# Differential scores: a second product over all 128 rows with zeros beside the keys' low parts, and a distance table loaded for each head

## The chip, the cores and the metric

The kernel runs on one core of a Trainium2 chip. The metric is the device time of one execution in microseconds (us): lower is better. Engines are named as the profile names them: PE (TensorE products), PEld (TensorE loads of the stationary operand, which lie beside PE), DVE (VectorE), ACT (ScalarE), POOL (GpSimd), SP (SyncE, which here only issues transfers; SPq is its queue).

## The reference, cut to what matters

A first block (adaptive norm, SSD and gated delta scans) is followed by a second block of two layers. Each layer projects 512 tokens of width 2048, runs a gated convolution, a differential attention and an attention to 256 memory tokens, and projects back. The change sits in the differential attention, six heads with two components of 64 features each:

```python
def diff_attention(q, k, v, lam, slopes):
    scale = DIFF_HALF_DIM ** -0.5
    ...
    def block(args):            # 128 queries
        qi, i = args
        qpos = (i * Q_BLOCK + jnp.arange(Q_BLOCK)).astype(jnp.float32)
        bias = -slopes[:, None, None] * jnp.abs(qpos[:, None] - key_pos[None, :])
        sc = jnp.einsum('bhcqd,bhckd->bhcqk', qi, kt).astype(jnp.float32) * scale + bias[None, :, None]
        p = jax.nn.softmax(sc, axis=-1).astype(vt.dtype)
        o = jnp.einsum('bhcqk,bhkd->bhcqd', p, vt)
        return o[:, :, 0] - lam.astype(o.dtype) * o[:, :, 1]
```

## The kernel before, in words

Products are made in the one-pass format float32r with operands split in two: a high part and a low part that holds what the high one leaves out. A projection takes three products for each tile: high by high, low by high, high by low. Weights come in pieces of 512 KB (128x1024) or 384 KB (128x768) through SP into `wr` (three buffers, `wpiece`); ACT makes the high part `wh` and DVE the low part `wl` (two buffers each); SP issues the next load when the `wl` of three pieces earlier is done. The order on each engine is fixed when the program is built.

In block 2 a layer (`layer`) runs two groups of three heads. For a group, `qk_group` projects the queries and then the keys of three heads token-major (`tm`), norms them, turns them feature-major (`qkT`) and stacks them for the scores: tile `q0` or `q1` (component c) holds the component's 64 query features' high parts in its own 64 rows (0 to 63 for c = 0, 64 to 127 for c = 1) and the low parts in the other 64; `k0` or `k1` holds the keys' high parts twice. One tile `kl` holds the low parts of both components' keys, each in its own rows. `v_group` makes the values.

`diff_head` then takes four chunks of 128 queries (qc). For a chunk and a component it issues two products into one PSUM tile `sc`: one over all 128 rows ([q high; q low] with [k high; k high]) and one over the component's 64 rows (q high with k low):

```python
nc.tensor.matmul(sc, lhsT=q[c][:, qs], rhs=k[c], start=True, stop=False)
nc.tensor.matmul(sc, lhsT=q[c][cs, qs], rhs=k[2][cs, :], start=False, stop=True)
```

So a chunk has a block of four score products on PE, and there are 2 layers x 6 heads x 4 chunks = 48 blocks. DVE adds the distance bias and takes the maximum (`p<-sc,bias`, with `mx`), ACT takes the exponentials, DVE combines the two components (`p<-p,c`). PE transposes the result (`pT`), ACT copies it out (`pTe`) and PE multiplies it with the values (`pv`); these steps are emitted one and two chunks later (`defer`), and in each chunk half a feature tile of other work (24 products `fm`, lines 176 to 178) is put between (`fill`). PSUM has four tiles for these (`g`) and four for projections (`mm`).

The bias of a head is a 128x896 tile with one buffer: POOL multiplies a resident table of distances (`dist`, loaded once from the constants `cst`) with the head's slope. Its buffer comes free when DVE has read the last chunk of the head before.

`mem_attention` reuses the tiles `k0`, `k1`, `q0`, `q1` for the memory's keys and values (`mk`, `mv`) and the tile `qktm` for its own queries.

Of the kernel before, what the change touches and what calls it, by code (L numbers as in the profile page):

```python
# [19 lines left out]
P = 128  # L20
# [5 lines left out]
# how far ahead of their place in the program the weights of each part are loaded and split  # L26
AHEAD = {"ada": 200, "mem": 300, "A": 300, "z": 300, "S": 300, "C": 150, "o1": 300, "tm": 300, "fm": 300, "o2": 300}
# half tiles of z projected at each place of block 1 where other work has waits to fill
ZFILL = {"keys": 2, "keys end": 2, "head": 1, "group": 2, "pair": (2, 2, 2, 4)}
# half tiles of the feature-major projection at each place of a layer's attention  # L30
FFILL = {"q": 2, "k": 2, "queries": 1, "mem q": 2, "mem queries": 1}
# adaLN steps before the constants, the memory's projections and the latent stream's loads come in
# [36 lines left out]
def lay_out(inp):  # L69
    """Orders the inputs for the chip: reshapes, transposes, concatenations and copies only."""  # L70
# [50 lines left out]
class K:  # L121
    def __init__(self, tc, I, out):
        self.tc, self.nc, self.I, self.out = tc, tc.nc, I, out
        # queues of the stores and of the loads of what was stored
        self.st, self.ld = tc.nc.scalar, tc.nc.sync
        self.queue = []
        self.part = "A"

    # ---------------------------------------------------------------- helpers
# [3 lines left out]
    def defer(self, *steps):  # L133
        """Emits the next step of each piece deferred so far, and takes the steps of a new one: what a step
        needs has time to come while other work is emitted in between."""
        self.advance()
        self.queue.append(list(steps))
# [29 lines left out]
    def proj_fm(self, outs, src, m=P, halves=(0, 1)):  # L167
        """ps[m, tok] = sum_k W[k, m] x[k, tok] for each (ps, x hi, x lo); src [2, P, 8*m]."""
# [11 lines left out]
    def proj_tm(self, pss, src, g, xh, xl):  # L180
        """pss[t][tok, g] = sum_k x[k, tok] W[k, g]; src [8, P, 2*g]."""
# [29 lines left out]
    def rsqrt_small(self, out, src, scale, n):  # L211
        """out = (src*scale + eps)^-0.5 on a small tile: a guess from the bits, a Newton and a Halley step."""
# [8 lines left out]
        # Newton's step leaves kappa times its value, so that Halley's needs no factor  # L221
# [12 lines left out]
    # ---------------------------------------------------------------- setup  # L234
    def first(self, out, src):
        """Load ahead of everything else."""
        with self.tc.high_priority(4000):
            self.nc.sync.dma_start(out=out, in_=src)
# [16 lines left out]
    def constants(self):  # L255
        """Constants and parameters of block 1, the lambda of the differential attention."""
# [19 lines left out]
        # halved convolution taps and bias (silu(x) = (tanh(x/2) + 1) * x/2)  # L276
# [18 lines left out]
    def rstd_cols(self, sq, n, width, out):  # L295
        """out[P, n/128] = (sum over partitions of sq / width + eps)^-0.5, tokens on partitions; sq may be parts of a sum."""
# [9 lines left out]
    def rstd_bcast(self, sq, n, width, out, cols=None):  # L306
        """out[P, n] = (sum over partitions of sq / width + eps)^-0.5, the same in every partition."""
        self.rstd_rows(self.rstd_diag(sq, n, width, self.tmp("rdiag")[:, :n], cols), out)

    def rstd_diag(self, sq, n, width, dg, cols=None):  # L310
        """rstd_cols in diagonal matrices."""
# [14 lines left out]
    # ---------------------------------------------------------------- adaLN  # L326
# [19 lines left out]
    def ada_chunk(self, cch):  # L346
        """Columns cch*1024 .. of the modulation of both streams, as per-partition columns (in steps)."""
        nc = self.nc
        pss = [self.psum("ch", "ada") for _ in range(2)]
        for k in range(KT):  # L350
            # one piece in four goes in whole, as float32: TensorE has the time, the split engines have not
# [29 lines left out]
    def gate_acc(self, i):  # L381
        """Partial sums over the features of quarter i of the latent stream's gate, c @ w_ada[:, 4096:]."""
# [12 lines left out]
    def gate_end(self, i, acc):  # L395
        """Columns of quarter i of the gate, times the post norm's gain."""
# [8 lines left out]
    # ---------------------------------------------------------------- memory keys and values  # L405
    def mem_prep(self):
        """hi and lo parts of the memory tokens and the columns of their norm, in steps."""
# [20 lines left out]
    def mem_proj(self, l, i, name):  # L428
        """Token-major product of the memory with block i of layer l's weights, whose rows take the norm's gain."""
# [22 lines left out]
    def mem_k(self, l):  # L452
        """Keys of the memory for layer l, feature-major, to DRAM, in steps."""
        nc = self.nc
        mkd = self.mkd[l] = self.dr.tile([P, 4, 256], F32, name=f"mkd{l}")
        # rms over the head in token-major form, then feature-major
# [24 lines left out]
    def mem_v(self, l):  # L481
        """Values of the memory for layer l, token-major, to DRAM, in steps."""
# [11 lines left out]
    # ---------------------------------------------------------------- modulated input of block 1  # L494
    def load_x(self):
        """Both streams and the sums of their squares, in steps."""
# [12 lines left out]
    def modulation(self):  # L509
        """The modulated inputs of both streams, in steps."""  # L510
# [23 lines left out]
    def modulate(self, half):  # L534
# [6 lines left out]
        if half == 0:  # L541
            # the context's tiles come first, so that theirs are the first places to be taken again
# [18 lines left out]
    def _affine(self, x, k, s):  # L561
        """x * (1 + scale) * gain + shift of feature tile k of stream s, in place."""
        self.nc.vector.tensor_scalar(out=x, in0=x, scalar1=self.am[:, k, s:s + 1], scalar2=self.mod[:, k, s:s + 1], op0=MUL, op1=ADD)

    # ---------------------------------------------------------------- block 1
    def targets(self, phs, name):
        """PSUM tiles of one projection for the given phases."""
        return [(self.psum("mm", name)[:, :ph.tok], ph.uh, ph.ul) for ph in phs]

    def small_proj(self, outs):  # L570
        """The 64 narrow outputs: rows 0-63 take W hi x hi + W hi x lo, rows 64-127 W lo x hi."""
# [17 lines left out]
    def tables(self, ph, ps):  # L589
        """Decay tables of one phase, token-major [P, column, chunk], and their rows."""  # L590
# [20 lines left out]
        # log1p(t) = 2 atanh(s), s = t / (2 + t)  # L611
# [42 lines left out]
        # dt * decay to the chunk's end (SSD columns)  # L654
# [1080 lines left out]
```

## Time and profile before

| | us |
|---|---|
| median of 3 runs | 3385.19 |
| lowest and highest run | 3374.1 and 3385.48 |
| span of the profiled execution, first to last instruction | 3380.9 |
| median of the runs less that span | 4.3 |

The profiled execution's own time is not listed apart from its span; the runs that are shown lie between 6.8 us below and 4.6 us above it. The page of the profile gives each engine's busy time in the span, and queries of the trace give single instructions with their start, their length and what they waited for. On PE the recorded lengths overlap, since products are pipelined: the time that one costs is the distance from its start to the next start.

### The profile page before, as it was taken

Reading aid. Unit: us, or ns where it says so; the run is one execution under the profiler, and the core shown is the slowest. Engines: PE = TensorE matmul, PEld = TensorE weight load, DVE = VectorE, ACT = ScalarE, POOL = GpSimd, SP = SyncE. Lnnn points to the kernel's source line nnn. Section 1 sums busy time; section 2 is a strip of 40 time slices with the busy share of each in tenths; the row PEclk is TensorE's granted clock in tenths of the full one; section 3 lists DMA queues with packets and bytes.
Section 4 is the critical chain, followed back from the end, with each engine's and each line's share of the span. In section 5 each row is a group of like instructions: output and inputs, shape, how many; then the busy total and the mean of one; then the engine's idle time right before and its main releaser. Section 6 shows DMA issues by size and latency. Waiting matters only on the chain.

```text
span 3380.9 us, 43409 instructions
## 1 busy us (share of the span) xinstructions
PE 3231.7 (96%) x16218; PEld 2665.5 (79%) x16218; DVE 1971.8 (58%) x3709; ACT 1228.0 (36%) x2371; POOL 481.8 (14%) x492
## 2 busy tenths in 40 slices
PE   7979989999999999997999999999999999999999
PEld 4637877787887887776888978888899798788887
DVE  7788887768667667666544464444344635544522
ACT  5644433334333333223333343323233434333311
POOL 1021220303424324012100010000110101000000
PEclk8989999999999999998999999999999999999999
DMA  8842342322322232754322322223433133122343
GB/s 313 283 172 86 130 134 84 107 99 89 106 77 70 79 103 76 251 186 143 103 79 74 115 73 88 76 93 131 146 109 108 57 101 110 63 88 81 107 149 106
DMA packets 169459, 392.57 MB, mean 116 GB/s; under 512 B 42784, under 2 KB 45344, under 8 KB 169248
## 3 DMA queue, kind: packets, MB, share of 16 engines
q1 hardware_dynamic: 140976, 341.02, 30.8%
q10 hardware_dynamic: 24432, 42.48, 3.3%
q0 software_dynamic: 3840, 6.29, 0.8%
q8 instruction: 128, 2.10, 0.3%
q14 instruction: 83, 0.68, 0.1%
HBM read 340.96 MB, written 42.47 MB: 113 GB/s over the span
## 4 chain that ended last, share of the span: by engine, by line
PE 52%; DVE 1%; issue 0%; ACT 0%; DVEq 0%; ACTq 0%
PE fm L178 7%; PE fm L176 7%; PE fm L177 7%; PE tm L192 4%; PE tm L191 4%; PE tm L190 4%; PE o L178 3%; PE o L177 3%; PE o L176 3%; PE pv L1490 2%; PE sc L1508 1%; PE sc L1507 1%; PE pT L209 1%; PE msc L1575 0%; PE qkT L1454 0%; PE oT L209 0%
## 5 line engine op out<-in xcount | busy, mean ns | idle before, releaser
L154 ACT CAST wh<-wr 128x1024 fp32r<-128x1024 f32 (+1 forms) x448 | 449.5, 1004 | 1328.5 <-PE fm L177 374.3
L155 DVE TENSOR_TENSOR wl<-wr,wh 128x1024 fp32r<-128x1024 f32 (+1 forms) x448 | 556.2, 1242 | 567.2 <-ACT wh L154 561.7
L176 PE MATMUL fm<-xh,wh 128*128 128x512 f32 x1088 | 431.5, 397 | 1.2 <-ACT qktm L1433 1.2
L178 PE MATMUL fm<-xh,wl 128*128 128x512 f32 x1088 | 426.1, 392 | 0.0
L177 PE MATMUL fm<-xl,wh 128*128 128x512 f32 x1088 | 425.1, 391 | 0.0
L192 PE MATMUL tm<-wh,xl 128*128 128x384 f32 (+1 forms) x896 | 308.3, 347 | 10.9 <-DVE xl L1409 10.7
L190 PE MATMUL tm<-wh,xh 128*128 128x384 f32 (+1 forms) x896 | 309.8, 346 | 3.9 <-ACT xh L1408 3.9
L191 PE MATMUL tm<-wl,xh 128*128 128x384 f32 (+1 forms) x896 | 308.6, 345 | 0.0
L176 PE MATMUL o<-yh,wh 128*128 128x512 f32 x768 | 299.7, 391 | 3.3 <-ACT yh L154 2.0
L178 PE MATMUL o<-yh,wl 128*128 128x512 f32 x768 | 299.8, 391 | 3.0 <-DVE wl L155 3.0
L177 PE MATMUL o<-yl,wh 128*128 128x512 f32 x768 | 299.6, 390 | 0.9 <-DVE yl L155 0.9
L178 PEld LDWEIGHTS fm<-xh,wl 128*128 128x128 f32 x1088 | 204.4, 188 | 42.9
L176 PEld LDWEIGHTS fm<-xh,wh 128*128 128x128 f32 x1088 | 204.6, 188 | 42.1 <-ACT qktm L1433 2.0
L177 PEld LDWEIGHTS fm<-xl,wh 128*128 128x128 f32 x1088 | 204.7, 188 | 39.8
L713 DVE SCALAR_TENSOR_TENSOR cacc<-cx,hcw,cacc 128x496 f32<-128x496 f32 (+2 forms) x248 | 165.4, 678 | 70.4 <-ACT cacc L706 67.2
L192 PEld LDWEIGHTS tm<-wh,xl 128*128 128x128 f32 x896 | 168.9, 189 | 20.5 <-DVE xl L1409 15.4
L190 PEld LDWEIGHTS tm<-wh,xh 128*128 128x128 f32 x896 | 169.7, 189 | 10.7 <-ACT xh L1408 5.5
L191 PEld LDWEIGHTS tm<-wl,xh 128*128 128x128 f32 x896 | 169.7, 189 | 4.8
L178 PEld LDWEIGHTS o<-yh,wl 128*128 128x128 f32 x768 | 144.2, 188 | 35.1 <-DVE wl L155 5.5
L176 PEld LDWEIGHTS o<-yh,wh 128*128 128x128 f32 x768 | 144.1, 188 | 34.7 <-ACT yh L154 3.4
L177 PEld LDWEIGHTS o<-yl,wh 128*128 128x128 f32 x768 | 144.2, 188 | 32.5 <-DVE yl L155 2.8
L176 PE MATMUL qkv<-uh,wh 128*128 128x512 f32 x384 | 154.8, 403 | 2.3 <-ACT wh L154 2.3
(523 smaller groups left out, 6229.7 us busy)
## 6 DMA issues: line engine op xcount, KB each, us to landing
wr<-w_fm SPq DMA_DIRECT2D x136, 512.0 KB
wr<-w_in SPq DMA_DIRECT2D x104, 512.0 KB
wr<-w_tm SPq DMA_DIRECT2D x96, 384.0 KB
ar<-w_ada SPq DMA_DIRECT2D x64, 512.0 KB
wr<-w_o SPq DMA_DIRECT2D x64, 512.0 KB
wr<-w_mkv SPq DMA_DIRECT2D x32, 512.0 KB
wr<-w_out SPq DMA_DIRECT2D x32, 512.0 KB
gw<-w_ada SPq DMA_DIRECT2D x64, 256.0 KB
```

The source lines that it names most:

```text
L154: nc.scalar.copy(hi, src)
L155: (eng or nc.vector).tensor_tensor(out=lo, in0=src, in1=hi.bitcast(F32), op=SUB)
L176: nc.tensor.matmul(ps, lhsT=hi[:, s], rhs=xh[kk], start=kk == 0, stop=False)
L177: nc.tensor.matmul(ps, lhsT=hi[:, s], rhs=xl[kk], start=False, stop=False)
L178: nc.tensor.matmul(ps, lhsT=lo[:, s], rhs=xh[kk], start=False, stop=kk == 15)
L190: nc.tensor.matmul(ps, lhsT=xh[kk][:, ts], rhs=hi[:, s], start=kk == 0, stop=False)
L191: nc.tensor.matmul(ps, lhsT=xh[kk][:, ts], rhs=lo[:, s], start=False, stop=False)
L192: nc.tensor.matmul(ps, lhsT=xl[kk][:, ts], rhs=hi[:, s], start=False, stop=kk == 15)
L209: self.nc.tensor.transpose(ps[:, m * P:(m + 1) * P], src[:, m * P:(m + 1) * P], self.C["ident"])
L713: nc.vector.scalar_tensor_tensor(out=av[:, :, o0:o1], in0=pv[:, :, o0 + d:o1 + d], scalar=w(k), in1=av[:, :, o0:o1], op0=MUL, op1=ADD)
L1490: self.nc.tensor.matmul(o[:, :P], lhsT=e[:, kc * P:(kc + 1) * P], rhs=v[kc][:, hs], start=kc == 0, stop=kc == n - 1)
L1507: nc.tensor.matmul(sc, lhsT=q[c][:, qs], rhs=k[c], start=True, stop=False)
```

## The change

The keys' low parts get a tile for each component (`kl0`, `kl1`, three buffers each), whose other 64 rows POOL sets to zero, and the second score product contracts all 128 rows: [q high; q low] with [k low; 0]. It takes the same stationary operand as the first. The resident table `dist` is gone; each head loads the distances into its own bias tile through SP (448 KB) and POOL multiplies them there in place. `qktm` shrinks to 384 columns, and the memory's queries move to the tiles `kl0` and `kl1`. The rest of the difference is comments.

```diff
@@ qk_group
-        tmt = self.wk.tile([P, 4, 512], F32, tag="qktm", name="qktm")[:, :, :384]
-        self.head_norm(pss, 6, 64, tmt)
+        tmt = self.wk.tile([P, 4, 384], F32, tag="qktm", name="qktm")
+        self.head_norm(pss, 6, 64, [tmt[:, t, :] for t in range(4)])
...
-            lo = self.wk.tile([P, 512], F32R, tag="t" if gain is None else "kl", name=f"{name}l")
+            if gain is None:
+                los = [self.wk.tile([P, 512], F32R, tag="t", name="ql")] * 2
+            else:
+                los = [self.wk.tile([P, 512], F32R, tag=f"kl{c}", name=f"kl{c}") for c in range(2)]
             for c in range(2):
-                r, o = slice(64 * c, 64 * c + 64), slice(64 - 64 * c, 128 - 64 * c)
+                r, o, lo = slice(64 * c, 64 * c + 64), slice(64 - 64 * c, 128 - 64 * c), los[c]
...
                     nc.gpsimd.dma_start(out=st[c][o], in_=st[c][r])
-            res.append((*st, lo))
+                    nc.gpsimd.memset(lo[o].bitcast(F32), 0.0)
+            res.append((st, los))
@@ diff_head
-        nc.gpsimd.tensor_scalar(out=bias, in0=self.dist, scalar1=-slope, scalar2=None, op0=MUL)
+        nm = len(NCONST) * P
+        nc.sync.dma_start(out=bias, in_=self.I["cst"][:, nm:nm + 896])
+        nc.gpsimd.tensor_scalar(out=bias, in0=bias, scalar1=-slope, scalar2=None, op0=MUL)
...
-                cs = slice(64 * c, 64 * c + 64)
                 sc = self.psum("g", "sc")
-                nc.tensor.matmul(sc, lhsT=q[c][:, qs], rhs=k[c], start=True, stop=False)
-                nc.tensor.matmul(sc, lhsT=q[c][cs, qs], rhs=k[2][cs, :], start=False, stop=True)
+                for i, kt in enumerate((k[0][c], k[1][c])):
+                    nc.tensor.matmul(sc, lhsT=q[0][c][:, qs], rhs=kt, start=i == 0, stop=i == 1)
@@ mem_attention
-        tma = self.wk.tile([P, 4, 512], F32, tag="qktm", name="mqtm")
-        tmt = [tma[:, t, :] for t in range(4)]
-        self.head_norm(pss, 4, P, tma)
+        tmt = [self.wk.tile([P, 512], F32, tag=f"kl{t % 2}", name="mqtm") for t in range(4)]
+        self.head_norm(pss, 4, P, tmt)
@@ block2
-            self.dist = cp.tile([P, 896], F32, name="dist")
-            self.nc.sync.dma_start(out=self.dist, in_=self.I["cst"][:, nm:nm + 896])
```

On PE no instruction changes its place; this is the difference at one chunk of the first layer's first head (`k_` tiles are the stacked keys of the two components, `kl` the low parts, `q_` the stacked queries, `vtm` the values):

```order
 L178 MATMUL fm<-xh,wl 128x512
-L1507 MATMUL sc<-k_14901,q_14516 128x512
-L1508 MATMUL sc<-kl,q_14516 128x512
-L1507 MATMUL sc<-k_14902,q_14517 128x512
-L1508 MATMUL sc<-kl,q_14517 128x512
-L1490 MATMUL pv<-vtm,pTe 128x128 x4
+L1514 MATMUL sc<-k_14899,q_14514 128x512
+L1514 MATMUL sc<-kl_14901,q_14514 128x512
+L1514 MATMUL sc<-k_14900,q_14515 128x512
+L1514 MATMUL sc<-kl_14902,q_14515 128x512
+L1495 MATMUL pv<-vtm,pTe 128x128 x4
 L209 MATMUL pT<-ident,p 128x128 x4
```

Four score products stand where four stood; only the tile of the low parts is another for each component.

On SP the loads of the table stand between loads of weights (`w_tm` and `w_fm` are pieces of the token-major and the feature-major projections); this is the difference over the first group of layer 0, from its beginning to the load for head 3:

```order
-L163 DMA wr<-w_fm 128x1024 x12
-L163 DMA wr<-w_tm 128x768 x8
+L163 DMA wr<-w_tm 128x768 x2
+L1503 DMA bias<-cst 128x896
+L163 DMA wr<-w_tm 128x768 x6
+L163 DMA wr<-w_fm 128x1024 x2
+L163 DMA wr<-w_tm 128x768 x8
+L163 DMA wr<-w_fm 128x1024 x8
+L1503 DMA bias<-cst 128x896
+L163 DMA wr<-w_fm 128x1024 x4
+L1503 DMA bias<-cst 128x896
+L163 DMA wr<-w_tm 128x768 x4
```

The weights keep their order among themselves; a load for heads 0, 1 and 2 has come in after two, 18 and 22 of them.

On POOL the zeros and the multiplications stand so in the changed kernel, from the transfers that double the first group's keys (`k_`) to the multiplications for heads 1 and 2 and the convolution's products `fe` and `ya`:

```order
L1471 DMA k_14933<-k_14933 64x512
L1471 DMA k_14900<-k_14900 64x512
L1471 DMA k_14917<-k_14917 64x512
L1472 MEMSET kl_14919 64x512
L1472 MEMSET kl_14935 64x512
L1471 DMA k_14934<-k_14934 64x512
L1472 MEMSET kl_14936 64x512
L1648 TENSOR_TENSOR ya<-ya,fe 128x512
L1472 MEMSET kl_16811 64x512
L1472 MEMSET kl_16812 64x512
L1504 TENSOR_SCALAR bias<-bias 128x896 x2
L1641 TENSOR_TENSOR fe<-fe 128x512
```

Before, the same stretch had the transfers in one run, `ya`, the two multiplications (from `dist`) and `fe`; the zeros have come in between.

## Rows read from the trace of the kernel before

**Rows 1.** The page: busy time, share of the span, instructions.

```profile
PE 3231.7 (96%) x16218; PEld 2665.5 (79%) x16218; DVE 1971.8 (58%) x3709; ACT 1228.0 (36%) x2371; POOL 481.8 (14%) x492
```

**Rows 2.** Windows: engines' busy time, PE clock, DMA share, in layer 0's first group.

```profile
1712.00:1816.00 104.00, 104.00 (x493) 79.83 (x492) 60.38 (x155) 46.81 (x110) 11.17 (x6) 1.00 0.19 61
```

**Rows 3.** Timeline of PE: start, length, instruction; first block of scores.

```profile
1712.67 0.33 PE L190 MATMUL tm<-wh,xh 128*128 128x384 f32 x1
1712.84 0.33 PE L191 MATMUL tm<-wl,xh 128*128 128x384 f32 x1
...
1713.19 0.40 PE L1507 MATMUL sc<-k,q 128*128 128x512 f32 x1
1713.51 0.50 PE L1508 MATMUL sc<-kl,q 64*128 64x512 f32 x1
1713.94 0.50 PE L1507 MATMUL sc<-k,q 128*128 128x512 f32 x1
1714.37 0.50 PE L1508 MATMUL sc<-kl,q 64*128 64x512 f32 x1
1714.81 0.50 PE L176 MATMUL fm<-xh,wh 128*128 128x512 f32 x1
1715.14 0.39 PE L177 MATMUL fm<-xl,wh 128*128 128x512 f32 x1
1715.37 0.39 PE L178 MATMUL fm<-xh,wl 128*128 128x512 f32 x1
```

**Rows 4.** Timeline of PEld there; in brackets the idle time before.

```profile
1714.37 0.18 PEld L1508 LDWEIGHTS sc<-kl,q 64*128 64x128 f32 x1 [0.25 <-issue]
...
1714.91 0.19 PEld L177 LDWEIGHTS fm<-xl,wh 128*128 128x128 f32 x1
```

**Rows 5.** Timeline of PE at the last of the 48 blocks.

```profile
2928.54 0.40 PE L1507 MATMUL sc<-k,q 128*128 128x512 f32 x1
...
2930.15 1.05 PE L1490 MATMUL pv<-vtm,pTe 128*128 128x128 f32 x7
```

**Rows 6.** Timelines of PE and ACT where head 1 begins.

```profile
1746.26 0.47 PE L1507 MATMUL sc<-k,q 128*128 128x512 f32 x1
...
1747.96 0.38 PE L1490 MATMUL pv<-vtm,pTe 128*128 128x128 f32 x1
...
1746.82 0.57 ACT L1483 COPY pTe<-pT 128x512 f32<-128x512 f32 x1
```

**Rows 7.** Timelines of SP, POOL, DVE and PE around head 1's bias.

```profile
1739.21 8.42 SPq L163 DMA_DIRECT2D wr<-w_fm  x2
...
1740.04 2.45 POOL L1497 TENSOR_SCALAR bias<-dist 128x896 f32<-128x896 f32 x1 [9.83 <-DVE mx L1512]
...
1747.32 0.69 DVE L1512 CUSTOM_DVE_ANT_0 p<-sc,bias 128x512 f32<-128x512 f32 x1
...
1751.42 0.75 DVE L1521 SCALAR_TENSOR_TENSOR p<-p,c 128x512 f32<-128x512 f32 x1
...
1756.05 0.66 PE L209 MATMUL pT<-ident,p 128*128 128x128 f32 x4
```

**Rows 8.** Windows around loads at heads 2 and 4; last figure GB/s.

```profile
1774.60:1776.60 2.00, 2.00 (x11) 1.62 (x10) 0.11 (x1) 1.86 (x5) 2.00 (x1) 1.00 0.83 270
...
1965.50:1972.60 7.10, 7.10 (x37) 5.93 (x38) 3.35 (x10) 2.66 (x8) 2.45 (x1) 1.00 0.65 222
```

**Rows 9.** The page: transfers, KB each, median us from issue to landing.

```profile
k<-k POOLq DMA_DIRECT2D x24, 128.0 KB, 2.9
```

**Rows 10.** Timelines of DVE and PE where head 4 begins.

```profile
1975.01 0.69 DVE L1512 CUSTOM_DVE_ANT_0 p<-sc,bias 128x512 f32<-128x512 f32 x1
...
1979.12 0.75 DVE L1521 SCALAR_TENSOR_TENSOR p<-p,c 128x512 f32<-128x512 f32 x1
...
1983.74 0.66 PE L209 MATMUL pT<-ident,p 128*128 128x128 f32 x4
```

**Rows 11.** Groups of POOL instructions: busy, mean ns.

```profile
L1643 POOL TENSOR_TENSOR ya<-ya,fe 128x512 f32<-128x512 f32 x12 | 15.3, 1279 | 288.1 <-DVE fe L1610 177.4 <-ACT wh L154 110.7
```

More of the change, by code (lines that the diff above doesn't have):

```diff
@@ L1432, in head_norm @@
         for t in range(4):
-            nc.scalar.activation(out=out[:, t, :], in_=pss[t], func=AF.Copy, scale=self.rc2[:, t:t + 1])
+            nc.scalar.activation(out=out[t], in_=pss[t], func=AF.Copy, scale=self.rc2[:, t:t + 1])
             j = self.wk.tile([P, 512], F32, tag="t", name="hj")[:, :n]
-            nc.scalar.activation(out=j, in_=out[:, t, :], func=AF.Square)
+            nc.scalar.activation(out=j, in_=out[t], func=AF.Square)
             nc.vector.tensor_reduce(out=ss[:, t * nseg:(t + 1) * nseg], in_=v(j), axis=AX.X, op=ADD)
@@ L1440, in head_norm @@
             rb = r[:, t * nseg:(t + 1) * nseg].rearrange("p (s o) -> p s o", o=1).to_broadcast([P, nseg, w])
-            nc.vector.tensor_tensor(out=v(out[:, t, :]), in0=v(out[:, t, :]), in1=rb, op=MUL)
+            nc.vector.tensor_tensor(out=v(out[t]), in0=v(out[t]), in1=rb, op=MUL)
     def qk_group(self, l, src, gain, name):
@@ L1648, in layer @@
         ys = [None] * 16
-        with self.work(f"wkL{l}", {"t": 5, "junk": 1, "qktm": 1, "vtm": 2, "q0": 3, "q1": 3, "k0": 3, "k1": 3, "kl": 3,
+        with self.work(f"wkL{l}", {"t": 5, "junk": 1, "qktm": 1, "vtm": 2, "q0": 3, "q1": 3, "k0": 3, "k1": 3, "kl0": 3, "kl1": 3,
                                    "bias": 1, "ao": 2, "fe": 2}):
@@ L1687, in block2 @@
         with ExitStack() as st:
-            cp = self.cp2
-            nm = len(NCONST) * P
-            self.dist = cp.tile([P, 896], F32, name="dist")
-            self.nc.sync.dma_start(out=self.dist, in_=self.I["cst"][:, nm:nm + 896])
             for l in range(2):
```

## The prediction, made before the changed kernel ran

> **What bounds the kernel now.** I read the page first, for the engine with the largest share: PE is busy in 96% of the span, DVE in 58%, ACT in 36%, POOL in 14% [rows 1]. A share over the whole span is an average over stages, so the next view is the table by windows over the stretch that the change touches, the three heads of layer 0's first group: PE is busy in all 104 of 104 us, at the full clock of 2.4 GHz (granted share 1.00), while DVE has 60 us and transfers take 0.19 of their engines [rows 2]. The other three groups read alike. The list of waits names no wait of PE there. So in these stretches the time is the sum of the distances between PE's starts, and whatever shortens one of them shortens the kernel, as long as nobody else becomes late.
>
> The timeline of PE then shows which distances are long. Products of 512 columns over 128 rows follow each other after 0.23 us (1715.14 to 1715.37). Inside a block of scores the four distances are 0.32, 0.43, 0.43 and 0.44 us, and the product behind the block is followed only after 0.33 [rows 3]. The timeline of the weight loads shows why: the load for a normal product starts while the product ahead of it is running (1714.91, for a product that starts at 1715.14), but the load for the 64-row product starts at 1714.37, with its own product, after PEld has idled 0.25 us [rows 3, 4]. So wherever a 64-row product and a 128-row product meet, the second one's load is not hidden. Each block has four such meetings: one between its first two products, two in the middle, one behind it.
>
> The Trainium skill ("TensorEngine Tiling (Array Packing)", Key Properties) says that a change of the tiling mode, not merely of the tile, drains TensorE. The rows agree with it: the distance grows by 0.20 us exactly where 64 and 128 rows alternate [rows 3].
>
> **The change part by part.**
>
> *The second product over 128 rows.* From the start of a block to the start of the product behind it, the first block takes 1.62 us [rows 3] and the last 1.61 [rows 5]. Forty of the 48 blocks lie at 1.60 to 1.62; the eight where a new head begins right behind transposes take 1.70 [rows 6]. That is 40 x 1.61 + 8 x 1.70 = 78.0 us. With 128 rows throughout I give all four products the normal 0.23: 48 x 4 x 0.23 = 44.2 us. The difference is 33.8 us. Behind the block the first distance is 0.33 in place of 0.23 [rows 3] where `fm` follows; where the 128-column products `pv` and `pT` follow I bound it by nothing and by the same 0.10, and take 0.07: 48 x 0.07 = 3.4 us. Together **37.2 us less** on PE. The multiplications by zero cost nothing of their own: a product's distance goes by its columns, and these stay 512.
>
> *What PE then runs into.* At the eight starts of a head behind another one, `pv` follows the block and needs `pTe`, which ACT ends at 1746.82 + 0.57 = 1747.39; the shortened block ends at 1746.26 + 0.92 = 1747.18 [rows 6]. ACT's work there hangs on products ahead of the block and doesn't move. So PE waits about 0.2 us and some time for the signal: 0.25 x 8 = **2 us back**.
>
> *The bias through SP.* It costs PE nothing unless DVE gets late. Before, POOL began when DVE had read the last chunk, at 1740.04, and the first use came at 1747.32 [rows 7]. Now at that time SP issues 448 KB and POOL's 2.45 us come behind their landing. The price of such a load: a 128 KB transfer lands 2.9 us after issue [rows 9]; 270 GB/s [rows 8] moves these in 0.5 us, so 2.4 us are for starting and landing, and 448 KB take 1.7 us. Landing at 1744.1 with nothing ahead; SP has issued a weight piece of 512 KB at 1739.21 [rows 7], which can hold the queue 2 us longer [rows 8], so 1746.1 at the latest. The bias is ready at 1746.6 to 1748.6. The first use would now come at about 1746.8, since one shortened block lies between. So DVE is late by 0 to 1.8 us. Behind it, `p<-p,c` ended at 1752.17 and PE asked for it with `pT` at 1756.05, a reserve of 3.9 us [rows 7], of which the two shortened blocks take 1.3: 2.6 remain and hide it. Heads 4 and 10 are worse: three loads of the memory's keys and values (256 KB each) and a weight piece stand ahead on the queue, which moves 1536 KB in 7.1 us there [rows 8]. The table ends (1280 + 448) / 1536 x 7.1 = 8.0 us after 1965.5, at 1973.5, or up to 2.4 later as a signal; POOL is done at 1976.0 to 1978.4, against a use at 1975.01 less 0.5 [rows 10]. DVE is 1.5 to 3.9 us late; the reserve is 1983.74 - 1979.87 = 3.9 less 1.3 [rows 10]. So PE waits 0 to 1.3 us there, and the next chunk may inherit some. Over the eight starts I bound this by 0 and 1.5 us each (12 us), and take **2 us**, nearer to nothing, because the reserve covers six of the eight. Heads 0, 3, 6 and 9 have whole projections between the load and its use.
>
> *SP's queue.* While the load of the table waits, what stands behind it on SP waits too: weight loads. In the order of the changed kernel the weight load behind each of the eight waits for a `wl` that DVE makes later than the chunk which frees the bias; the two issues around head 1 lie 8.1 us apart (1739.21 and 8.42 us on, less 0.33 for the issue itself) [rows 7], and the table is issued between them. So this costs nothing; its cover is that gap.
>
> *The zeros, the smaller tiles.* The 24 memsets of 64x512 on POOL are shown by no row; between nothing and the 1.28 us of POOL's two-input operation of the same columns [rows 11]. Four of them stand among the transfers of a group's keys, at most 5 us; the values' projection of 30 us lies between these and the first score product. In POOL's order nothing else of use stands behind them, so zero. The memory's queries in `kl0` and `kl1` wait for score products that are long past, and dropping the single early load of the table frees nothing that is waited for.
>
> Sum: 3380.9 - 37.2 + 2 + 2 = 3347.7 for the profiled execution's span; the median of the runs lies 4.3 above that span, which gives **3352 us**, 1.0% less.
>
> **The rivals.**
>
> *No gain (A).* The long distances come not from the 64 rows but from two products sharing the stationary operand and the PSUM tile. Both stay, so the blocks keep 1.61 us and the time is 3385, up to 3387 with the table's waits. Against it: `tm` lines 190 and 191 share their stationary operand and lie 0.17 us apart at 384 columns, and the three `fm` products share one PSUM tile at 0.23 [rows 3]. For it: no row shows two 128-row score products in sequence. The Trainium skill ("TensorE: Matmul & The Clock Gate", Part 3: Packing small matmuls — row/col tiling) speaks for A: it lets a weight load overlap a running product only where the row groups differ, and gives a product of few rows the same time as one of 128. By that, 128-row products would hide no load and little would be won. The trace differs: loads of 128 rows start under 128-row products, as row 1714.91 shows [rows 4].
>
> *Half the gain (B).* DVE's lateness is passed on from chunk to chunk and PE waits 2 us at each of the eight starts: 16 us in place of 2, 3366. For it, the bias now has 1.7 us of moving and 2.4 us of latency in a chain that had neither; against it, DVE is idle 40% there [rows 2] and catches up.
>
> *Slower (C).* SP's queue: if the table's load holds back the weight piece behind it, PE misses weights. It decides from 37.2 / 8 = 4.7 us at each start; a piece's whole turn of 8.1 us [rows 7] at each would give 3385 - 37 + 65 = 3413. Against it stands the order of the waits above; three pieces of lead lie between.
>
> **How the numbers follow.** The forecast has 0.80, A 0.08, B 0.08, C 0.04. A measurement of this kernel tells about 0.5% (17 us) from no change. Faster by more: the forecast and half of B, 0.84. Within: A and the other half, 0.12. Slower: C, 0.04. Range: with 0.10 behind every block and no waits the saving is 38.6, 3347; the runs before reach 11 us below their median, and a new median may lie up to nine of these lower: 3338. Above, B's 3366 is the end. So 3338 to 3366.
>
> **What would show it.** In the profile after: the score products 0.23 us apart and the load of each under the product ahead; PE's busy time about 35 us less at the same count; POOL's multiplication waiting for a DMA and ending about 7 to 9 us behind the last use, 10 at heads 4 and 10; PE without waits of more than 1 us at `pT`. The prediction is wrong if the distances stay at 0.43 (A), if PE waits for `p` through the bias (B), or if ACT's `wh` waits for loads (C).

## The result, and the profile of the changed kernel

The changed kernel takes 3346.2 us (median of 4 runs, 3342.56 to 3348.36), the kernel before 3379.64 beside it on the same chip (4 runs, 3373.94 to 3385.48): a ratio of 0.9898, with a 95% interval from 0.9881 to 0.9915. The forecast was 3352. The profiled execution took 3348.36 us, with a span of 3346.6.

The page of the changed kernel, busy time and count of each engine, against [rows 1]:

```profile
PE 3195.9 (95%) x16218; PEld 2668.9 (80%) x16218; DVE 1969.3 (59%) x3709; ACT 1230.9 (37%) x2371; POOL 493.2 (15%) x516
```

The same 16218 products keep PE busy 35.8 us less. The window over layer 0's first group (PE, PEld, DVE, ACT, POOL, PE clock, DMA share, GB/s) answers to [rows 2]:

```profile
1712.00:1816.00 104.00, 104.00 (x543) 89.25 (x542) 60.54 (x156) 49.36 (x113) 12.21 (x8) 1.00 0.25 82
```

PE is still busy for all of the 104 us, at the same granted clock, and gets 543 products through it in place of 493. Nothing was idle there that was filled: the same work stands closer together. Where, the timelines of PE and of its weight loads show, for the first block of scores and the first product of the last one [rows 3 to 5]:

```profile
1713.61 0.39 PE L1514 MATMUL sc<-k,q 128*128 128x512 f32 x1
1713.84 0.39 PE L1514 MATMUL sc<-kl,q 128*128 128x512 f32 x1
1714.07 0.39 PE L1514 MATMUL sc<-k,q 128*128 128x512 f32 x1
1714.29 0.40 PE L1514 MATMUL sc<-kl,q 128*128 128x512 f32 x1
1714.53 0.39 PE L176 MATMUL fm<-xh,wh 128*128 128x512 f32 x1
1714.76 0.40 PE L177 MATMUL fm<-xl,wh 128*128 128x512 f32 x1
...
2895.19 0.39 PE L1514 MATMUL sc<-k,q 128*128 128x512 f32 x1
...
1714.07 0.19 PEld L1514 LDWEIGHTS sc<-kl,q 128*128 128x128 f32 x1
1714.30 0.19 PEld L176 LDWEIGHTS fm<-xh,wh 128*128 128x128 f32 x1
```

Every distance is now 0.22 to 0.24 us, the one behind the block too. The load for the fourth product starts at 1714.07, when the third product starts, and not with its own product at 1714.29; before, it started with its own after PEld had idled 0.25 us [rows 4].

From the first product of the first block to the first product of the last, 1713.61 to 2895.19, are **1181.58 us**; before they were 1215.35 (1713.19 to 2928.54, [rows 3, 5]). This **stretch** is 33.77 us shorter, and the whole span 34.3. It is the best measure here, as the experiments show: where the first block starts differs from one profiled kernel to the next (1706.04 to 1721.97), nearly all of it by work that no edit touches, but two kernels with the same blocks have the same stretch to 0.01 us.

Head 1's start, PE and ACT, against [rows 6]:

```profile
1743.60 0.48 PE L1514 MATMUL sc<-k,q 128*128 128x512 f32 x1
...
1744.38 0.40 PE L1514 MATMUL sc<-kl,q 128*128 128x512 f32 x1
1744.78 0.60 PE L1495 MATMUL pv<-vtm,pTe 128*128 128x128 f32 x3
...
1744.16 0.57 ACT L1488 COPY pTe<-pT 128x512 f32<-128x512 f32 x1
```

The last distance is 0.40 and not 0.23: `pv` starts 0.05 us after ACT has ended `pTe`. The path of the bias, with SP, POOL, DVE and PE at head 1 (and DVE and PE at head 4), against [rows 7, 10]:

```profile
1737.83 0.93 SPq L1503 DMA_DIRECT2D bias<-cst  x1
1742.77 2.45 POOL L1504 TENSOR_SCALAR bias<-bias 128x896 f32<-128x896 f32 x1 [6.35 <-DMA bias<-cst]
1745.26 0.69 DVE L1518 CUSTOM_DVE_ANT_0 p<-sc,bias 128x512 f32<-128x512 f32 x1 [0.48 <-POOL bias L1504]
1748.68 0.75 DVE L1527 SCALAR_TENSOR_TENSOR p<-p,c 128x512 f32<-128x512 f32 x1
1752.17 0.60 PE L209 MATMUL pT<-ident,p 128*128 128x128 f32 x4
...
1964.71 0.69 DVE L1518 CUSTOM_DVE_ANT_0 p<-sc,bias 128x512 f32<-128x512 f32 x1 [0.47 <-POOL bias L1504]
1968.13 0.75 DVE L1527 SCALAR_TENSOR_TENSOR p<-p,c 128x512 f32<-128x512 f32 x1
1971.26 0.60 PE L209 MATMUL pT<-ident,p 128*128 128x128 f32 x4
```

POOL now waits for the transfer and DVE for POOL, but DVE only 0.48 us. Behind it `p<-p,c` ends at 1749.43, and PE asks for it at 1752.17: a **reserve** of 2.7 us is left at head 1, and 2.4 at head 4 (1971.26 less 1968.88). At the third head of a group it is smaller, 1.8 us at head 5 (2002.93 less 2001.18); over the eight starts it lies between 1.75 and 2.9, 2.2 on the mean. PE waits for nothing at these `pT`.

### The profile page after: what moved, and what is told of

It reads as the page before. It is cut to its first block, busy times and chain, and to the rows that moved or that the text cites. A ratio compares the mean times of both kernels' runs of the same rounds, so it can differ in the third digit from the quotient of the medians.

```text
span 3346.6 us, 43464 instructions
## 1 busy us (share of the span) xinstructions
PE 3195.9 (95%) x16218; PEld 2668.9 (80%) x16218; DVE 1969.3 (59%) x3709; ACT 1230.9 (37%) x2371; POOL 493.2 (15%) x516
## 4 chain that ended last, share of the span: by engine, by line
PE 51%; DVE 1%; issue 0%; ACT 0%; DVEq 0%; ACTq 0%
PE fm L178 7%; PE fm L176 7%; PE fm L177 7%; PE tm L192 4%; PE tm L190 4%; PE tm L191 4%; PE o L176 3%; PE o L178 3%; PE o L177 3%; PE pv L1495 2%; PE sc L1514 1%; PE pT L209 1%; PE msc L1580 0%; PE qkT L1454 0%; DVE xl L1409 0%; PE oT L209 0%
```

## The experiments

The theory: before, TensorE lost time wherever a 64-row and a 128-row product met; with one shape the loads are hidden, and the loads of the table are covered by DVE's reserve. Rivals: the gain or a part of it comes from another edit; the 64-row product is dear by itself; the table's loads do cost something, which the gain outweighs. The stretch is in the last column, in us; before 1215.35, changed 1181.58. A time from one run alone is marked.

| kernel | median us | before beside it | ratio and interval | stretch |
|---|---|---|---|---|
| one table per layer | 3349.9 | 3381.49 | 0.9907 [0.9892, 0.9922] | 1181.59 |
| loads, without the padded product | 3382.78 | 3381.49 | 1.0004 [0.9993, 1.0016] | 1215.36 |
| before, 64-row products side by side | 3355.36 | 3381.49 | 0.9926 [0.991, 0.9941] | 1186.49 |
| 64 rows only, halves alternating | 3345.35 (one) | 3381.49 | | 1177.49 |
| 64 rows only, written half by half | 3347.46 (one) | 3384.5 | | 1177.62 |
| bias one pass later | 3358.3 (one) | 3384.5 | | 1186.49 |
| bias two passes later | 3381.89 | 3384.5 | 0.9984 [0.9974, 0.9994] | 1218.73 |
| third 128-row product | 3367.89 | 3384.5 | 0.9946 [0.9929, 0.9962] | 1200.47 |
| three pairs of 64 rows | 3368.14 | 3384.03 | 0.9948 [0.993, 0.9967] | 1197.14 |

**One table per layer.** The padded product without the loads: the tile is loaded once a layer, and each head scales the head before's bias in place.

```diff
-        bias = self.wk.tile([P, 896], F32, tag="bias", name="bias")
...
-        nc.sync.dma_start(out=bias, in_=self.I["cst"][:, nm:nm + 896])
-        nc.gpsimd.tensor_scalar(out=bias, in0=bias, scalar1=-slope, ...)
+        if h == 0:
+            self.bias = self.wk.tile([P, 896], F32, tag="bias", name="bias")
...
+            nc.sync.dma_start(out=self.bias, in_=self.I["cst"][:, nm:nm + 896])
+        bias = self.bias
+        nc.gpsimd.tensor_scalar(out=bias, in0=bias, scalar1=-slope if h == 0 else 2.0 ** (-8.0 / 6), ...)
```

> The padded product without the eleven further loads of the table: one bias tile per layer is loaded once and each head multiplies it by the ratio of two slopes (2^-1.33) in place. Theory (a 64-row product beside a 128-row one leaves a weight load uncovered, 0.20 us at each meeting): the gain is the product's alone, so the ratio to the kernel before is as for the change, 0.988 to 0.992, blocks of four score products 0.92 us and 1.17 us at the eight head starts; POOL ends about 4 to 6 us earlier behind the last use than with loads. Rival (part of the 34 us comes from the loads, the freed table or the moved tiles): ratio above 0.994. Second rival (the loads cost something hidden in the change): ratio below 0.987.

Ten of the twelve loads are gone, and the stretch is 1181.59 against 1181.58. What POOL's `bias` operation waits for is counted in the view of its tile, first in the changed kernel, then here (us, times):

```profile
  DMA bias<-cst: 173.2, 11
```

```profile
  DVE mx L1520: 156.1, 10
...
  DMA bias<-cst: 5.2, 2
```

POOL is released by DVE's last chunk again, as before the change, and DVE no longer waits for POOL; neither is worth anything to the end. **The loads cost no time that can be measured**, and the gain is the product's.

**Loads, without the padded product.** The changed kernel with the 64-row product back in place.

```diff
-                for i, kt in enumerate((k[0][c], k[1][c])):
-                    nc.tensor.matmul(sc, lhsT=q[0][c][:, qs], rhs=kt, start=i == 0, stop=i == 1)
+                cs = slice(64 * c, 64 * c + 64)
+                nc.tensor.matmul(sc, lhsT=q[0][c][:, qs], rhs=k[0][c], start=True, stop=False)
+                nc.tensor.matmul(sc, lhsT=q[0][c][cs, qs], rhs=k[1][c][cs, :], start=False, stop=True)
```

> The change without its product: the second product contracts the component's 64 rows again, while the table is loaded for each head, the zeros are written and the tiles are split and moved as in the change. Theory: blocks go back to 1.61 and 1.70 us, ratio 0.999 to 1.001 (at most 2 us for late biases). Rival (the other edits bring or cost time): ratio below 0.997 or above 1.003.

PE's timeline at its first block has the distances of [rows 3] again:

```profile
1712.74 0.40 PE L1514 MATMUL sc<-k,q 128*128 128x512 f32 x1
1713.07 0.50 PE L1515 MATMUL sc<-kl,q 64*128 64x512 f32 x1
1713.49 0.50 PE L1514 MATMUL sc<-k,q 128*128 128x512 f32 x1
```

Loads, zeros, smaller tiles and the memory's other places together are worth 0.01 us in the stretch. With the run above this closes the question of which edit it is.

**Before, 64-row products side by side.** The same four products with the same operands, in another order: 128, 128, 64, 64 rows.

```diff
+            scs = [self.psum("g", "sc") for _ in range(2)]
+            for c in range(2):
+                nc.tensor.matmul(scs[c], lhsT=q[c][:, qs], rhs=k[c], start=True, stop=False)
...
-                sc = self.psum("g", "sc")
-                nc.tensor.matmul(sc, lhsT=q[c][:, qs], rhs=k[c], start=True, stop=False)
-                nc.tensor.matmul(sc, lhsT=q[c][cs, qs], rhs=k[2][cs, :], start=False, stop=True)
+                nc.tensor.matmul(scs[c], lhsT=q[c][cs, qs], rhs=k[2][cs, :], start=False, stop=True)
...
```

> The kernel before with the four products of a block in another order: both 128-row products, then both 64-row ones (rows 0 to 63, rows 64 to 127); the same four products. Theory (each meeting of 64 and 128 rows costs): two meetings in place of four; distances 0.23, 0.33, 0.23, 0.43 us, block 1.22 us in place of 1.61, so about 19 us less, ratio 0.994; if the two 64-row products in different halves run side by side, third distance near 0.05 and up to 28 us less, 0.992. Rival (each 64-row product costs 0.2 us on either side by itself, whatever its neighbour): block 1.6 us, ratio 1.000.

PE and PEld at its second block (x2 marks two instructions in one row):

```profile
1714.51 0.62 PE L1506 MATMUL sc<-k,q 128*128 128x512 f32 x2
1715.06 0.50 PE L1509 MATMUL sc<-kl,q 64*128 64x512 f32 x2
1715.49 0.66 PE L209 MATMUL pT<-ident,p 128*128 128x128 f32 x4
...
1715.06 0.19 PEld L1509 LDWEIGHTS sc<-kl,q 64*128 64x128 f32 x2 [0.36 <-issue]
1715.49 0.42 PEld L209 LDWEIGHTS pT<-ident,p 128*128 128x128 f32 x4 [0.25 <-issue]
```

The block takes 0.98 us (1714.51 to 1715.49) in place of 1.61. Two meetings are left, and PEld idles at just these two. Reordering alone gives 28.86 of the 33.77 us, without a zero, a load or another tile. Two things are in this: the two 64-row products, in different halves of the rows, start together (x2 at 1715.06), which saves one distance of 0.23 in each of the stretch's 47 blocks, an estimated 10.8 us; the other 18 are the two meetings that are gone, near the 19 expected for these alone. So a 64-row product is not dear by itself; what is dear is to go from one shape to the other.

**64 rows only.** Two kernels in which both products of a component contract 64 rows, the one with the halves alternating by hand, the other as the loop writes it, half by half. The first:

```diff
+            scs = [self.psum("g", "sc") for _ in range(2)]
+            for i in range(2):
+                for c in range(2):
+                    cs = slice(64 * c, 64 * c + 64)
+                    nc.tensor.matmul(scs[c], lhsT=q[c][cs, qs], rhs=(k[c], k[2])[i][cs, :], start=i == 0, stop=i == 1)
...
```

> The kernel before with only 64-row products: the first product too contracts the component's 64 rows, which leaves out the queries' low part; order component 0, 1, 0, 1, so that the halves of the array alternate. Theory (meetings cost, 64-row products among themselves don't): distances inside the block at most 0.23 us, the uncovered load only at the block's two edges, block with both edges 1.1 to 1.3 us, about 15 to 20 us less than before; if halves run side by side, two of the distances near 0.05 and the block under 1.0. Rival (a 64-row product costs 0.2 us by itself): four distances of 0.43, block 1.7 us, no gain.

The second:

```diff
-                nc.tensor.matmul(sc, lhsT=q[c][:, qs], rhs=k[c], start=True, stop=False)
+                nc.tensor.matmul(sc, lhsT=q[c][cs, qs], rhs=k[c][cs, :], start=True, stop=False)
                 nc.tensor.matmul(sc, lhsT=q[c][cs, qs], rhs=k[2][cs, :], start=False, stop=True)
```

> The kernel before with both products of a component on 64 rows: the first one contracts the 64 rows of the queries' and keys' high parts alone, so the product of the queries' low parts is left out of the scores. Order as before: two products in the lower half of the rows, then two in the upper half. With the order in which the halves alternate, each pair of different halves began at one moment and a pair took 0.33 us, 34.4 us for the 48 blocks. The theory (the cost of before lay in each meeting of a 64-row and a 128-row product, a product of 64 rows costs no more than one of 128, and loads lie beside products of the same half too): inside the block 0.23, then 0.00 (the halves change), then 0.23, about 0.5 us, with a meeting of 0.3 to 0.4 on each side, 0.66 to 0.7 for a block. Rival (a load waits for the product before it where both use the same rows): 0.4 us or more between two products of one half, a block of 0.9 us or more and a time above 3350.

PE and PEld of the second at its third block, where line 1507 and line 1508 alternate in the program:

```profile
1729.60 0.50 PE L1507 MATMUL sc<-k,q 64*128 64x512 f32 x2
1729.93 0.40 PE L1508 MATMUL sc<-kl,q 64*128 64x512 f32 x2
1730.26 0.49 PE L1490 MATMUL pv<-vtm,pTe 128*128 128x128 f32 x2
...
1729.59 0.19 PEld L1507 LDWEIGHTS sc<-k,q 64*128 64x128 f32 x2 [0.35 <-issue]
1729.70 0.19 PEld L1508 LDWEIGHTS sc<-kl,q 64*128 64x128 f32 x2
```

Both blocks take 0.66 us, and the stretch is 37.9 and 37.7 us shorter than before, where 15 to 20 were expected of the first kernel. For the second, both ideas about the inside were wrong: neither 0.23 in one half and then the other, nor a load that waits. The two products of line 1507, one in each half, start 0.01 us apart, although a product of line 1508 stands between them in the program; then the two of line 1508 start, 0.33 us later. The order in which the halves are written makes no difference (1177.49 and 1177.62). The Trainium skill ("TensorEngine Tiling (Array Packing)", Key Properties) says that different tiles can load and multiply in parallel, and these rows agree, at 0.01 us. Another page of the Trainium skill ("TensorE: Matmul & The Clock Gate", Part 3: Packing small matmuls — row/col tiling) has products start in the order of the program; here the third starts ahead of the second, so the measurement differs. The passages remain: 0.32 us ahead of the block in place of 0.23, and PEld idle on both sides.

**The bias later.** GpSimd scales the table in two passes, then in three, each 2.45 us.

```diff
-        nc.gpsimd.tensor_scalar(out=bias, in0=bias, scalar1=-slope, scalar2=None, op0=MUL)
+        nc.gpsimd.tensor_scalar(out=bias, in0=bias, scalar1=-1.0, scalar2=None, op0=MUL)
+        nc.gpsimd.tensor_scalar(out=bias, in0=bias, scalar1=slope, scalar2=None, op0=MUL)
```

> The change, with the distance table scaled in two passes of GpSimd instead of one, so that the bias of a head is ready one pass later; a pass took 2.45 us in the profile of the change. The theory: the bias of a head there was late by 0.7 us at head 1 and 1.1 us at head 4, and behind the first block VectorE still ended 2.7 and 2.4 us ahead of the transpose that needs it, so one pass more about uses up the reserve: the first p of a head comes some 2.4 us later, TensorE waits 0 to 0.5 us at a head's start, and the time stays within 4 us of the changed kernel's 3346. Rival one (VectorE's lateness at a start passes to TensorE in full, as the half-gain case of the prediction has it): 8 x 2.4 = 20 us more, 3366. Rival two (the reserve is far larger than what the first block shows): no wait at all, and none in the next run with two more passes either.

One pass: the stretch is 4.9 us longer. PE's waits between 1700 and 2930 us (total, times, longest):

```profile
PE pT L209 <- DVE p L1528: 3.4, 5, 1.4
```

The reserve holds most of it: 3.4 us of wait from 8 x 2.45 = 19.6 us of delay. The 4.9 us are more than the 4 expected, and the time from one run is 12 us above the changed kernel's; 5.0 of these lie ahead of the first block, which starts at 1718.57 in place of 1713.61, a place that scatters as much between other kernels. For the three passes the edit has two lines with the factor -1.0 ahead of the old one.

> The change, with three passes of GpSimd over the distance table instead of one: the bias of a head is ready 4.9 us later. The theory (a reserve of 2.4 to 2.7 us behind the first block of a head, and TensorE the bound): TensorE waits 4.9 - 2.5 = 2.4 us at each of the eight starts, 19 us in all, a time near 3365 and a ratio to the kernel before near 0.995. Rival (a larger reserve, since VectorE and TensorE may catch up over the head's other blocks): no more than 4 us above the change. Rival (no reserve): 8 x 4.9 = 39 us more, 3385, no gain left.

The stretch is 37.2 us longer, twice what the theory gave, and the number is that of the rival without a reserve (39). But the waits say otherwise. PE's waits there, and its timeline at head 2:

```profile
PE pT L209 <- DVE of L225: 11.5, 4, 2.9
PE pT L209 <- DVE p L1529: 10.1, 4, 2.7
PE sc L1516 <- DVE mx L1520: 1.9, 2, 0.9
...
1782.55 0.39 PE L1516 MATMUL sc<-kl,q 128*128 128x512 f32 x1
1785.83 0.63 PE L209 MATMUL pT<-ident,p 128*128 128x128 f32 x4 [2.88 <-DVE of L225]
...
1788.74 0.63 PE L176 MATMUL fm<-xh,wh 128*128 128x512 f32 x1
1789.17 0.63 PE L177 MATMUL fm<-xl,wh 128*128 128x512 f32 x1
```

Line 225 is a small step of a norm that ends just behind `p<-p,c`. PE waits at the first `pT` of each of the eight heads, 2.9 and 2.5 us on the mean of the first two rows, 21.6 us together, near the theory's 19; with the third row 23.5. Behind the wait at 1785.83 the same products lie 0.43 us apart (1788.74 to 1789.17) in place of 0.23. The windows say why (PE's and the other engines' busy time, then the granted clock):

```profile
1786.00:1790.00 4.00, 4.00 (x14) 3.19 (x13) 3.73 (x11) 1.48 (x4) 0.00 (x0) 0.57 0.02 4
1790.00:1800.00 10.00, 10.00 (x54) 8.49 (x53) 6.42 (x15) 4.44 (x11) 1.27 (x1) 1.00 0.26 79
...
2016.00:2022.00 6.00, 5.39 (x26) 4.57 (x27) 4.84 (x17) 2.32 (x6) 0.00 (x0) 1.00 0.20 61
2646.00:2652.00 6.00, 5.82 (x21) 4.76 (x22) 4.78 (x18) 2.31 (x6) 0.00 (x0) 0.72 0.13 30
```

After PE's wait the granted clock is 0.57 on the mean of 4 us, most of them at 1.2 GHz in place of 2.4, with PE busy all the time. This is so behind six of the eight waits, and not by their length alone: behind head 5's wait of 2.88 us (to 2016.61) and head 1's of 2.59 the clock stays at 1.00, behind head 7's of 1.99 (to 2646.18) it falls; what decides was not followed. Seven of 23 windows of 20 us over the heads stand at 0.89 to 0.94; one less their shares, times 20, adds up to 12.4 us. With 23.5 of waits that is 35.9 of the 37.2; the list counts a wait from the recorded end of the product ahead, 0.40 us behind its start and not 0.23, which makes some 1.7 us more over the ten. So the theory's reserve was about right and its price incomplete, and by the time alone the wrong theory would have won.

**Third 128-row product.** The keys' low parts once more in each component.

```diff
-                for i, kt in enumerate((k[0][c], k[1][c])):
+                for i, kt in enumerate((k[0][c], k[1][c], k[1][c])):
...
```

> The change, with a third 128-row product for each component of a block (the keys' low parts beside zeros once more, so the low parts count twice in the scores). It prices the product that the change substitutes, by itself. The theory (a product of 128 rows by 512 columns behind another of 128 rows takes 0.23 us of TensorE, its load hidden, and TensorE is the bound): the blocks become 6 x 0.23 = 1.38 us, 96 x 0.23 = 22 us more, less up to 8 x 0.25 = 2 us that the wait for pTe at the head starts gives back: 3366 to 3368, ratio 0.995 to 0.996. Rival (TensorE has room in these stretches, and what was taken out of before was the meetings' wait and not TensorE's time): less than 10 us more. Rival (a load does not lie beside products of the same stationary shape): 0.4 us each, 38 us more.

PE at its second block:

```profile
1724.64 0.39 PE L1514 MATMUL sc<-k,q 128*128 128x512 f32 x1
1724.87 0.62 PE L1514 MATMUL sc<-kl,q 128*128 128x512 f32 x2
1725.33 0.40 PE L1514 MATMUL sc<-k,q 128*128 128x512 f32 x1
```

Three products in 0.69 us. The stretch is 18.9 us longer, against 20 to 22: TensorE has no room in these stretches, and the padded product costs the 0.23 us that the sum took for it.

**Three pairs of 64 rows.** From the runs above: all three exact products of a component on its own half, from the kernel before.

```diff
+            for i, (a, b) in enumerate(((0, 0), (0, 1), (1, 0))):
+                for c in range(2):
+                    cs = slice(64 * c, 64 * c + 64)
+                    nc.tensor.matmul(scs[c], lhsT=q[a][cs, qs], rhs=k[b][cs, :], start=i == 0, stop=i == 2)
...
```

> The kernel before with all three products of a component on 64 rows of the component's own half: high by high, high by low, low by high, written so that the halves alternate, six products for a block. Queries and keys then need one tile of high and one of low parts each, without a copy into the other half; the distance table stays resident and nothing is padded. Nothing is left out of the scores. The theory (two 64-row products in different halves begin together, a pair takes 0.33 us, and each passage between 64 and 128 rows costs 0.1 us ahead of the block and 0.05 to 0.1 behind it): a block takes 3 x 0.33 = 0.99 us, 16 us more over the 48 blocks than the two pairs of the run without the low part (span 3343.6), so a span near 3359 and a ratio near 0.993 to 0.995, behind the change's 0.9898. Rival (the third pair is hidden or starts without waiting, 0.23 us a pair): a block of 0.7 to 0.8 us, a span below 3352, no worse than the change. Rival (the copies that fall away were worth time too): shorter still than its blocks say.

PE at its second block, and its list of waits over the heads:

```profile
1728.53 0.49 PE L1502 MATMUL sc<-kh,qh 64*128 64x512 f32 x2
1728.86 0.39 PE L1502 MATMUL sc<-kl,qh 64*128 64x512 f32 x2
1729.09 0.40 PE L1502 MATMUL sc<-kh,ql 64*128 64x512 f32 x2
1729.42 0.65 PE L209 MATMUL pT<-ident,p 128*128 128x128 f32 x4
...
PE pT L209 <- DVE mx L1508: 8.4, 10, 1.3
```

The stretch is 15.6 us longer than the changed kernel's, where 16 were expected, but again the inside differs. The pairs follow after 0.33 and then 0.23 us: 0.33 is what the first pair takes, not a pair. The block is 0.89 us, shorter than the changed kernel's 0.92. What it loses stands around it: over the 48 blocks the distances ahead add up to 14.2 us in place of 9.4 and those behind to 9.4 in place of 6.4, and PE waits 8.4 us for DVE at `pT`. By the distances these ten waits cost about 10.4, as the list counts a wait from the recorded end of the product ahead; with this the sum comes out. At one of the longest (1803.54) PE goes on when DVE has ended its first pass over a chunk's scores (1803.47), which stands behind a `wl` of 2.33 us; why in this order was not followed. It beats the kernel before, and not the changed one.

The padded product with the table kept resident was not run; the run with one table per layer stands for it. No version here that makes all the products beats the changed kernel; the two with 64 rows only have a stretch some 4 us shorter, and leave one product out.

## Why the prediction was right, step by step

| step | predicted us | measured us |
|---|---|---|
| blocks of scores | 78.0 to 44.2, and 2 back for `pTe`: -31.8 | 78.0 to 46.1: -31.9 |
| product behind a block | -3.4 | 9.4 to 6.4: -3.0 |
| bias through SP, wait of PE | +2 (0 to 12) | 0 |
| SP's queue, zeros, smaller tiles | 0 | 0.01 (loads without the product) |
| span | 3347.7 | 3346.6 |
| median less span | +4.3 | -0.4 |

*What bounds it, and the meetings.* Right, and shown from both sides: by taking two of the four meetings out without touching a product (some 18 of the 28.86 us), and by adding a product (18.9 us). The 0.20 us "exactly where 64 and 128 rows alternate" is the mean and not each: [rows 3] have 0.09, 0.20, 0.20 and 0.21 over the normal 0.23 inside the block and 0.10 behind it, 0.80 for the four meetings. Rival A falls with the first block above: the two products still share the stationary operand and the PSUM tile, and lie 0.23 us apart.

*The wait for `pTe`.* The 2 us came, made of two parts: 0.17 us at each of the eight starts for `pTe`, and 0.09 for the first product behind transposes (0.32 in place of 0.23), which was there before (1.70 in place of 1.61) and which the sum had dropped. That they meet 0.25 is luck.

*Behind the block.* `fm` 0.23 in place of 0.33, `pv` 0.11 in place of 0.21, `pT` and `oT` (the transposes of a head's output) 0.11 in place of 0.16: the full 0.10 where `fm` and `pv` follow, half of it at the transposes. Eight of the `pv` keep 0.21, at the heads' starts.

*The bias.* Right in that PE waits for nothing, but the sizes were off on both sides. The bias came at the early end of its bounds: POOL ends 2.01 us behind the start of head 4's first block (1964.68 less 1962.67), where the sum had 2.0 to 4.4 (1976.0 and 1978.4, less 1973.96), and 6.9 to 7.9 us behind the last use at all eight starts, where 10 were expected at heads 4 and 10. In the run with one table per layer, where the bias is never late, DVE's first use lies 0.94 us behind the block's start at both heads; here it is 1.66 at head 1 and 2.03 at head 4, so 0.7 and 1.1 us late, where I had 0 to 1.8 and 1.5 to 3.9. The reserve without that lateness is 3.2 us at these two heads in that run, more than the 2.6 of the sum; 2.7 and 2.4 are what the lateness leaves of it, and that they lie near 2.6 is chance. So the 2 us were a mis-sized term, whose measured value is nothing, and rival B does not come in. Half of its mechanism is real: with the bias 4.9 us later PE waits at all eight starts. But it waits there once, at heads 4 and 10 twice, and at no later chunk, and B's price was incomplete: on 21.6 us of wait at `pT` came some 12 by the granted clock.

*Rival C.* The stretch of the kernel that has the loads and not the product is that of before: nothing behind the table on SP's queue was late for PE.

*The median.* The larger part of the 5.8 us between 3352 and 3346.2 is the last step: I took the 4.3 us between the profiled span of before and the median of its three runs as if it belonged to the kernel. One run more (3373.94) puts that median at 3379.64, 1.3 below the same span; in the changed kernel the median lies 0.4 below. A run takes 1.7 to 2.3 us longer than its own span, and the rest is scatter. The two kernels' spans differ by 34.3, as the sum had it to 1.1; as the start of the first block scatters by far more, and happened to lie within 0.4 us in these two, this closeness is partly luck. The blocks and what follows them, 34.9 against 35.2 us, are what the sum can be held to.

## What to carry to other kernels

Where TensorE is the bound, read the distance between starts and not the length of a product, and look for places where the shape of the stationary tile changes: there a load is not hidden. Keep one shape (with zeros, if need be), or put the products of the odd shape next to each other, in different halves of the rows, which here brought 85% of the gain without a further tile. Before new work goes into a side chain, measure its reserve at the first consumer on the bound engine, at every start and not at one, and count beyond it not only the wait but the clock behind the wait.

## What the runs showed of the hardware that was not expected

- Two 64-row products in different halves of the rows start 0.01 us apart, and the second may come from behind another product in the program. At 512 columns a pair holds PE for 0.23 us where another pair stands on both sides; the first, behind 128-row products, holds it for 0.33, and so does the last, ahead of 128 rows.
- A wait of 2.88 us on PE was followed by some 4 us at a granted clock of 0.57, another of 2.88 was not (1.00 over the next 5 us), and one of 1.99 was, by 6 us at 0.72; behind waits up to 1.4 us, in the run with one pass more, the clock stayed at 1.00.
- The stretch of 1181.58 us between two marks in the program was repeated to 0.01 us by another kernel with the same blocks, while the time ahead of the first mark differed by up to 16 us among the eleven kernels.
